# The entry of three FFNs: norm, sums of x, first weights and covered tiles put in one given order

## Chip, cores and metric

The kernel runs on one core of a Trainium2 chip. The metric is device time in microseconds of one execution of the whole program. TensorE (PE) multiplies matrices into PSUM banks, VectorE (DVE) and ScalarE (ACT) do elementwise work, GpSimd (POOL) and SyncE (SP) mostly issue transfers here.

## What is computed

A decoder trunk of two layers on 512 tokens of width 1024, all in float32:

```python
for l in range(DEPTH):                                   # DEPTH = 2
    x = x + 0.5 * swiglu(rms_norm(x, ffn1_norm[l]), ffn1_w_in[l], ffn1_w_out[l])
    h = rms_norm(x, mix_norm[l]) @ w_mix_in[l]           # three token mixers share this projection
    y = concat(short_conv(...), hgrn2(...), forgetting_attention(...))
    x = x + y @ w_mix_out[l]
    x = x + 0.5 * swiglu(rms_norm(x, ffn2_norm[l]), ffn2_w_in[l], ffn2_w_out[l])

def swiglu(h, w_in, w_out):                              # D_FF = 2816
    gate, up = jnp.split(h @ w_in, 2, axis=-1)
    return (jax.nn.silu(gate) * up) @ w_out
```

So there are four FFNs in the program: FFN1 and FFN2 of layer 0, FFN1 and FFN2 of layer 1. The two FFN2 stand directly behind a mixer; FFN1 of layer 1 stands behind FFN2 of layer 0. Only the first FFN has a different opening (it reads x from memory).

## The kernel before

**Numbers in two parts.** Every float32 operand of a matmul is kept as a high part (a copy rounded to float32r, made by ScalarE) and a low part (the rest, a subtraction on VectorE). A product is three matmuls: high x high, high x low, low x high (`mm3`, lines 327, 333, 334; its `hl` tiles hold weights, `x` or `xc` tiles the activations). Weights come in by transfers into `st` tiles (two buffers) or `w` tiles, and their two parts go into `hl` tiles (three buffers), by `granule` and `parted` (lines 315 and 316) or `prepare` (lines 696 and 698).

**Covered tiles and halved products.** The hidden width 2816 is 22 tiles of 128. At the start of an FFN the first tiles (6 in the first FFN, 4 in the other three) are computed plainly, in pairs: one covered pair is a `stream` over the 8 tiles of x's rows, in four granules of two row tiles each, 96 matmuls of 512 columns. They are called covered because beside them the norm and the operands of what follows are made. The rest is done by a scheme with seven products of half size in place of eight (named P1 to P7): `plan` writes the sequence of products and the steps between them, `halved` runs it, `product` is 24 matmuls of 256 columns. For it the activations are needed as quarters (4 tiles of x by 256 tokens), scaled by gain and the norm, and as sums of quarters; each of the seven has its own high and low part, `xc` (`halves_of_x`, lines 594, 600, 629 to 634). The sequence of an input product is P1, P2, P6, P5, P7, P3, P4; products use banks a, c, a, b, a, b, a, and ScalarE copies bank a (`g`) after P1 and P6 and bank b (`u`) after P5, before the bank is added to again.

**The norm.** The sum of squares (`sqa`) is brought across partitions by a matmul with `ones_mean` (line 427 in `norm`, called inside the first covered pair), then Ln, Exp, a square on ScalarE and three VectorE steps give `inv` (`end_norm`, `rsqrt`).

**What sets the order.** Tile dependencies give the waits. Beyond them a scheduler places instructions by priority, unless `follow` chains an instruction to the one before it on its engine ("a", "v", "p" and so on): chained instructions keep the order in which the code writes them. In `halved` all is chained. In the entry (`cover`, `halves_of_x`, `finish`) of before almost nothing is, and weight parts of covered tiles have high priority. `finish` turns a covered tile's two banks into its hidden values: two multiplies by `inv` (lines 554, 555), a silu, two multiplies into `hq` quarters (lines 573, 576).

**The split pass.** In every P1 of an input product the first matmul is done as two of 128 columns (`parted` in `mm3`), the rest as one of 256.

Of the kernel before, what the change touches and what calls it, by code (L numbers as in the profile page):

```python
# [8 lines left out]
F32 = mybir.dt.float32  # L9
F32R = mybir.dt.float32r  # L10
# [4 lines left out]
ALU = mybir.AluOpType  # L15
# [22 lines left out]

AHEAD_LOAD, AHEAD_SUM = 4, 4


# [17 lines left out]
def plan(covered):  # L59

    into = lambda c: [
# [15 lines left out]
    def between(a, b, *what):  # L82

        loose.append((max(a, 0), max(b, 0), what))
# [78 lines left out]
class Trunk:  # L163
# [32 lines left out]
    def build_consts(self, scratch):  # L196

        nc = self.nc
# [84 lines left out]
    def granule(self, parts, kk, ahead=True, skew=0):  # L283
# [14 lines left out]
        with self.tc.high_priority() if ahead else ExitStack():  # L298
            hi, lo = self.parted(st[:, : kk * c], 1 if ahead else kk, skew)
# [3 lines left out]
    def parted(self, src, pieces=1, skew=0):  # L303

        nc = self.nc
        n = src.shape[1]
        hl = self.wp.tile([P, 2 * 1024 + 64], F32R, tag="hl", name=self.n("hl"), bufs=3)  # L310
        hh, ll = (hl[:, a + skew : a + skew + n] for a in (0, 1024))
        w = n // pieces
        for c in range(0, n, w):
            hi, lo = hh[:, c : c + w], ll[:, c : c + w]
            a = nc.scalar.copy(hi, src[:, c : c + w])  # L315
            b = nc.vector.tensor_sub(lo, src[:, c : c + w], hi)  # L316
            if pieces > 1:
                self.follow("a", a)
                self.follow("v", b)
        return hh, ll  # L320

    def mm3(self, acc, ah, al, bh, bl, first, last, parted=False, keep=False):

        nc = self.nc
        n = bh.shape[-1]
        for c in (slice(0, n // 2), slice(n // 2, n)) if parted else (slice(0, n),):
            i = nc.tensor.matmul(  # L327
                acc[:, c], ah, bh[:, c], start=first and c.start == 0, stop=False,
                skip_group_check=True,
            )  # L330
            if keep:
                self.follow("p", i)
        nc.tensor.matmul(acc, ah, bl, start=False, stop=False, skip_group_check=True)  # L333
        i = nc.tensor.matmul(acc, al, bh, start=False, stop=last, skip_group_check=True)  # L334
        if keep:
            self.follow("p", i)
# [4 lines left out]

    def stream_steps(self, jobs, parts_of, act, nk, mid=None, pre=None):

        k = 0
        while k < nk:
# [5 lines left out]
            skew = SKEW_MOVING if jobs[0][2] is not None and jobs[0][0].shape[-1] < T else 0  # L359
            rows = self.granule(parts_of(k, kk), kk, pre is None, skew)  # L360
            end = k + kk == nk
# [30 lines left out]
    def norm_part(self, j, pool, xj=None, part=None):  # L392

        nc = self.nc
# [21 lines left out]

    def rsqrt(self, out, v, r, t):

        nc = self.nc
        self.act(t, r, AF.Square)  # L420
        nc.vector.scalar_tensor_tensor(out=t, in0=v, scalar=EPS, in1=t, op0=ALU.add, op1=ALU.mult)  # L421
        nc.vector.tensor_scalar(t, t, scalar1=-0.5, scalar2=1.5, op0=ALU.mult, op1=ALU.add)
        nc.vector.tensor_mul(out, r, t)

    def end_norm(self, bank, pool):
# [5 lines left out]
        self.act(r, bank, AF.Ln, bias=self.epsc)  # L431
        self.act(r, r, AF.Exp, scale=-0.5)
        self.inv = self.res.tile([P, T], F32, tag="inv", name=self.n("inv"))
        self.rsqrt(self.inv, bank, r, t)


    def ffn(self, w_in, w_out, next_gain, covered, begin=None, out=None):

        nc = self.nc
        tc = self.tc
        with tc.tile_pool(name=self.n("ffn"), bufs=1) as fp:
            self.tt, self.tb = "g2", 2
            if begin is not None:
                x, gain, logits = begin
            self.hq = {}
            halved = self.halved(fp, w_in, w_out, covered)
            finish = self.cover(fp, w_in, covered, begin, halved)
            for n, _ in enumerate(halved):  # L450

                if n in (1, 3):
                    finish(n // 2)

# [41 lines left out]
    def cover(self, fp, w_in, covered, begin, then):  # L496

        nc = self.nc
# [45 lines left out]

    def finish(self, fp, f, i, pg, pu, keep):

        nc = self.nc  # L550
# [3 lines left out]
        V(nc.vector.tensor_mul(gi, pg, self.inv))  # L554
        V(nc.vector.tensor_mul(ui, pu, self.inv))
        A(self.act(gi, gi, AF.Silu))
        a, k = divmod(f + i, 4)
        for b in range(2):
            V(self.hidden(self.quarter(fp, 0, a, b)[:, k, :], *(t[:, 256 * b : 256 * b + 256] for t in (gi, ui)), a != b))

    def quarter(self, fp, c, a, b):


        if (c, a, b) not in self.hq:
# [5 lines left out]
    def hidden(self, out, g, u, other):  # L570

        if other:
# [5 lines left out]
    def halves_of_x(self, fp):  # L578

        nc = self.nc
# [38 lines left out]
    def two(self, hi, lo, src, other):  # L624

        nc = self.nc
# [9 lines left out]
    def halved(self, fp, w_in, w_out, covered):  # L636

        nc = self.nc  # L650
# [5 lines left out]
        def src(u, q):  # L656

            kind, w = u
# [10 lines left out]
        def add(u, q, q2):  # L669

            G(nc.gpsimd.dma_start(raw[u, q], src(u, q2), accum_op=ALU.add))

        def total(u, name):

            q = lambda i: raw[u, i]
# [24 lines left out]
        def moving(c, p):  # L700

            hi, lo = (
# [42 lines left out]
        for q in (2, 0, 3, 1):  # L745
# [3 lines left out]
            S(nc.sync.dma_start(t, src(u, q)))  # L749
        add(u, 2, 3)  # L750
        yield
        total(u, "S2")
        for s in seq[: LEAD - 1]:
            prepare(*s)()
        run(-1)
# [10 lines left out]
        for n, (kind, w, p) in enumerate(seq):  # L766
# [68 lines left out]
    def lower_bounds(self, logits, scratch):  # L835

        nc = self.nc
# [53 lines left out]
    def mix(self, l, w, w_out, conv_w, out_gain, q_gain, k_gain, f_bias, next_gain):  # L891
# [3 lines left out]
        with tc.tile_pool(name=self.n("mix"), bufs=1) as mp:  # L895
# [23 lines left out]
            def features_steps(spans, banks, mid=None):  # L919

                bs = [self.bank(t) for t in banks]
# [13 lines left out]
            def tokens(a, banks=("mm", "mm")):  # L935

                bs = [self.bank(t) for t in banks]
# [78 lines left out]
            with tc.tile_pool(name=self.n("at"), bufs=1) as ap_:  # L1016
# [37 lines left out]
                def most():  # L1054

                    for dg in range(4):
# [52 lines left out]
    def hgrn(self, l, pr, hp, z, q, q2, v, sg, og):  # L1109

        nc = self.nc
# [175 lines left out]
    def fox_decay(self, mp, zf):  # L1293

        nc = self.nc
# [24 lines left out]
    def fox_qkv(self, mp, hf, tokens, half):  # L1320


        nc = self.nc
# [28 lines left out]
    def fox_prep(self, pool, h, qk, g):  # L1352

        nc = self.nc
# [106 lines left out]
    def turn_x(self):  # L1464

        nc = self.nc
# [15 lines left out]
    def open_x(self, x, gain, fp, k, loaded=False):  # L1482

        if not loaded:
# [16 lines left out]
    def load_x(self, x, j, fp):  # L1501

        nc = self.nc
# [10 lines left out]
def trunk_kernel(  # L1514
# [6 lines left out]
    for l in range(DEPTH):  # L1521
        k.ffn(
            ffn1_w_in[l], ffn1_w_out[l], mix_norm[l], 4 if l else 6,
            begin=(x, ffn1_norm[0], hgrn_lb_logits) if l == 0 else None,
# [38 lines left out]
```

## Time and profile before

| | us |
|---|---|
| median of 3 runs | 1865.98 |
| runs | 1869.36, 1865.98, 1865.92 |
| span of the profiled execution | 1868.0 |
| the run that can hold that span (the other two are shorter than it) | 1869.36 |
| TensorE busy | 1837.1 (98%) |
| VectorE busy | 1481.9 (79%) |
| ScalarE busy | 1009.8 (54%) |

A row of a profile's timeline gives the start, the length, the engine, the line of the kernel, the operation, what it writes and reads with their shapes, and in brackets how long the engine stood idle before it and what it then waited for. Matmuls overlap: the distance between two starts is the pace, not the length. A window row gives, for each stretch of time, busy time and count of instructions per engine, then the clock granted to TensorE (1.00 is full), the share of the transfer engines and GB/s.

### The profile page before, as it was taken

How to read it: one execution, taken by the hardware profiler on the slowest of the kernel's cores; microseconds unless marked ns; L12 is line 12 of the kernel's file. 1: busy time of each engine (PE TensorE's matmuls, PEld its weight loads, DVE VectorE, ACT ScalarE, POOL GpSimd, SP SyncE). 2: the span in 40 equal slices, each digit the busy share in tenths (PEclk: the TensorE clock that was granted, in tenths of full speed). 3: DMA queues.
4: the chain of work that ended last, by engine and by line, in shares of the span. 5: the costliest groups of instructions: out<-in, count | busy, mean ns of one | idle time of the engine just before them, and what ended most of it. 6: DMA issues, size and time to landing. Idle time of an engine off the chain costs nothing.

```text
span 1868.0 us, 33432 instructions
## 1 busy us (share of the span) xinstructions
PE 1837.1 (98%) x13559; PEld 1707.5 (91%) x13559; DVE 1481.9 (79%) x2101; ACT 1009.8 (54%) x1467; POOL 177.4 (9%) x182
## 2 busy tenths in 40 slices
PE   8999999999999999999999999999999999999999
PEld 6899999899878799999889999988998777999997
DVE  7889787677887978878697887867768878888883
ACT  4455554564676545555455555545547654555552
POOL 0011120100000011112001111201000000021210
PEclk9999999999999999999999999999999999999999
DMA  7658783332323757868265786823323237577662
GB/s 203 169 119 189 181 178 92 74 92 69 80 80 95 216 105 170 189 171 170 79 202 129 167 191 171 170 63 91 78 61 90 80 107 204 147 155 196 147 137 90
DMA packets 245418, 251.91 MB, mean 135 GB/s; under 512 B 19568, under 2 KB 230000, under 8 KB 245264
## 3 DMA queue, kind: packets, MB, share of 16 engines
q1 hardware_dynamic: 191664, 183.69, 33.1%
q0 software_dynamic: 53600, 66.09, 22.2%
q8 instruction: 106, 1.74, 0.4%
q14 instruction: 48, 0.39, 0.1%
HBM read 223.98 MB, written 2.10 MB: 121 GB/s over the span
## 4 chain that ended last, share of the span: by engine, by line
PE 85%; DVE 8%; ACT 3%; issue 2%; DMA 2%; SPq 0%; ACTq 0%; DVEq 0%
PE mm L327 12%; PE mm L334 12%; PE mm L333 12%; PE sc L327 6%; PE sc L334 6%; PE sc L333 6%; PE pt L327 6%; PE pt L333 6%; PE pt L334 6%; PE po L327 3%; PE po L333 3%; PE po L334 3%; DVE hl L316 1%; DMA st<-in_ffn_w_in_dram 1%; ACT hl L315 1%
## 5 line engine op out<-in xcount | busy, mean ns | idle before, releaser
L696 ACT CAST hl<-w 128x1024 fp32r<-128x1024 f32 x322 | 337.6, 1049 | 338.0 <-PE mm L334 80.7
L698 DVE TENSOR_TENSOR hl<-w,hl 128x1024 fp32r<-128x1024 f32 x322 | 392.9, 1222 | 104.9 <-ACT hl L696 104.9
L316 DVE TENSOR_TENSOR hl<-st,hl 128x512 fp32r<-128x512 f32 (+2 forms) x196 | 166.7, 852 | 117.6 <-ACT hl L315 116.4
L315 ACT CAST hl<-st 128x512 fp32r<-128x512 f32 (+2 forms) x196 | 146.6, 750 | 189.4 <-PE mm L334 67.8
L327 PE MATMUL mm<-xc,hl 128*128 128x256 f32 (+1 forms) x741 | 202.1, 276 | 1.1 <-ACT g L796 1.1
L333 PE MATMUL mm<-xc,hl 128*128 128x256 f32 x728 | 201.9, 277 | 0.0
L334 PE MATMUL mm<-xc,hl 128*128 128x256 f32 x728 | 201.2, 276 | 0.0
L334 PE MATMUL sc<-xc,hl 128*128 128x256 f32 x528 | 148.4, 281 | 8.7 <-DVE hl L698 8.7
L327 PE MATMUL sc<-xc,hl 128*128 128x256 f32 (+1 forms) x538 | 148.9, 280 | 0.6 <-ACT g L796 0.5
L333 PE MATMUL sc<-xc,hl 128*128 128x256 f32 x528 | 148.5, 281 | 0.0
L327 PEld LDWEIGHTS mm<-xc,hl 128*128 128x128 f32 x741 | 138.3, 188 | 1.6 <-ACT g L796 1.5
L334 PEld LDWEIGHTS mm<-xc,hl 128*128 128x128 f32 x728 | 136.9, 188 | 0.0
L333 PEld LDWEIGHTS mm<-xc,hl 128*128 128x128 f32 x728 | 136.7, 188 | 0.0
L327 PE MATMUL pt<-xc,hl 128*128 128x256 f32 (+1 forms) x488 | 133.1, 275 | 0.0
L333 PE MATMUL pt<-xc,hl 128*128 128x256 f32 x480 | 133.0, 277 | 0.0
L334 PE MATMUL pt<-xc,hl 128*128 128x256 f32 x480 | 132.6, 276 | 0.0
L327 PE MATMUL mm<-hl,x 128*128 128x256 f32 (+1 forms) x384 | 112.4, 293 | 1.0 <-DVE ft L421 0.4
L334 PEld LDWEIGHTS sc<-xc,hl 128*128 128x128 f32 x528 | 101.5, 192 | 9.1 <-DVE hl L698 9.1
L327 PE MATMUL mm<-x,hl 128*128 128x512 f32 x272 | 109.7, 403 | 0.0
L334 PE MATMUL mm<-hl,x 128*128 128x256 f32 (+1 forms) x384 | 107.5, 280 | 0.0
L333 PE MATMUL mm<-hl,x 128*128 128x256 f32 (+1 forms) x384 | 107.2, 279 | 0.0
L334 PE MATMUL mm<-x,hl 128*128 128x512 f32 x272 | 106.6, 392 | 0.0
(470 smaller groups left out, 5695.1 us busy)
## 6 DMA issues: line engine op xcount, KB each, us to landing
w<-in_ffn_w_in_dram SPq DMA_DIRECT2D x140, 512.0 KB, 5.2
w<-in_ffn_w_out_dram SPq DMA_DIRECT2D x64, 512.0 KB, 4.5
w<-in_ffn_w_out_dram POOLq DMA_DIRECT2D x56, 512.0 KB, 8.5
st<-in_w_mix_in_dram SPq DMA_DIRECT2D x88, 256.0 KB, 2.8
st<-in_ffn_w_in_dram SPq DMA_DIRECT2D x72, 256.0 KB, 3.2
w<-in_ffn_w_in_dram POOLq DMA_DIRECT2D x35, 512.0 KB, 8.1
w<-S POOLq DMA_DIRECT2D x35, 512.0 KB, 4.7
st<-in_ffn_w_out_dram SPq DMA_DIRECT2D x24, 512.0 KB, 3.6
```

The costliest lines, as they stand in the source:

```text
L315: a = nc.scalar.copy(hi, src[:, c : c + w])
L316: b = nc.vector.tensor_sub(lo, src[:, c : c + w], hi)
L327: i = nc.tensor.matmul(acc[:, c], ah, bh[:, c], start=first and c.start == 0, stop=False, skip_group_check=True,)
L333: nc.tensor.matmul(acc, ah, bl, start=False, stop=False, skip_group_check=True)
L334: i = nc.tensor.matmul(acc, al, bh, start=False, stop=last, skip_group_check=True)
L696: A(nc.scalar.copy(hi, src))
L698: return lambda: V(nc.vector.tensor_sub(lo, src, hi))
```

## The change

For the three FFNs other than the first, the entry is a new function, `enter`, in place of `cover` and `halves_of_x`. It does the same operations, and chains ScalarE's and VectorE's in the order written: the norm, then x's quarters and sums in the order P1, P2, P5, P6 with the weight parts of the second covered pair between them, then the first sum of weights and the first two products' weights. `stream_steps` gets a `given` argument: a granule for which it holds is chained, and the generator stops after making it, ahead of its matmuls. P7, P3, P4 and the covered tiles' hidden values are left for `entry`, a table by product number that `halved` calls behind its products (0, 1, 2, 3, 5, 6, 8, 9). The norm's matmul now stands after the third granule of the first covered pair, and the first four transfers of the halved products are issued ahead of the second pair's second granule. Apart from that, the first pass of P1 is split only at the first pair of each of the three chunks and at the first halved pair. `finish` is divided in `clear` and `values`.

```diff
+FIRST = 6
...
     def stream_steps(self, jobs, parts_of, act, nk, mid=None, pre=None, given=None):
...
+            keep = given is not None and given(k)
+            rows = self.granule(parts_of(k, kk), kk, pre is None, skew, keep)
+            if keep:
+                yield
...
+            if begin is None:
+                self.enter(fp, w_in, halved)
+                for _ in halved:
+                    pass
...
+    def enter(self, fp, w_in, then):
...
+        ba = self.next4()
+        first = stream(0, ba, lambda k: k == KD - 2)
+        for _ in range(4):
+            next(first)
+        nb = self.bank("pt" if self.ntog % 2 == 0 else "po")
+        bb = self.next4()
+        second = stream(2, bb, lambda k: True)
+        self.ngain = self.const.tile([P, KD], F32, tag="ngain", name=self.n("ngain"))
+        A(nc.scalar.activation(self.ngain, self.gain, AF.Copy, scale=-1.0))
+        next(second)
+        self.end_norm(nb, fp, True)
+        self.table(SILU)
+        next(first, None)
+        next(then)
...
+        quarter(0, 0)
+        high("P1")
+        quarter(1, 0)
+        lows["P1"]()
+        next(second)
+        next(second)
+        high("P2")
+        quarter(0, 1)
+        lows["P2"]()
+        quarter(1, 1)
+        add((0, 0), (0, 1))
+        high("P5")
+        next(second)
+        next(second)
+        clear(0, 0)
+        lows["P5"]()
+        add((0, 0), (1, 1))
+        high("P6")
+        next(second)
+        next(second)
+        next(second, None)
+        self.given["total"]()
+        lows["P6"]()
+        self.given["prepare"](0)
+        self.given["prepare"](1)
+        clear(0, 1)
+        add((0, 1), (1, 1))
+        next(then)
+        self.entry = {
+            0: lambda: (high("P7"), values(0, 0), lows["P7"]()),
+            1: lambda: (values(0, 1), high("P3")),
+            2: lambda: (lows["P3"](), add((0, 0), (1, 0))),
+            3: lambda: both("P4"),
+            5: lambda: clear(2, 0),
+            6: lambda: values(2, 0),
+            8: lambda: clear(2, 1),
+            9: lambda: values(2, 1),
+        }
...
-            product(u, p, acc, p in new, p in ("P2", "P3", "P4"), kind == "I" and p == "P1")
+            product(
+                u, p, acc, p in new, p in ("P2", "P3", "P4"),
+                kind == "I" and p == "P1" and w in (covered, *(f0 for f0, _ in CHUNKS)),
+            )
+            if n in self.entry:
+                self.entry.pop(n)()
```

In `enter`, `quarter` is four multiplies on VectorE, `high` a copy on ScalarE, `low` the rest on VectorE, `add` a sum of two quarters on VectorE, and `next(second)` alternately makes a granule's weight parts and issues its matmuls.

More of the change, by code (lines that the diff above doesn't have):

```diff
@@ L297, in granule, with parted @@
             at += w
[L298 to L299 removed]
+        with self.tc.high_priority() if ahead and not keep else ExitStack():
+            hi, lo = self.parted(st[:, : kk * c], 1 if ahead else kk, skew, keep)
         h3, l3 = (a.rearrange("p (k c) -> p k c", k=kk) for a in (hi, lo))
         return [(h3[:, i, :], l3[:, i, :]) for i in range(kk)]
[L303 removed]
+    def parted(self, src, pieces=1, skew=0, keep=False):
         nc = self.nc
@@ L415, in norm_part, with rsqrt, end_norm @@
             nc.vector.tensor_add(self.sqacc, self.sqacc, sq)
-    def rsqrt(self, out, v, r, t):
+    def rsqrt(self, out, v, r, t, keep=False):
         nc = self.nc
[L420 to L425, printed above, removed]
+        A, V = ((lambda i, e=e: self.follow(e, i)) if keep else (lambda i: i) for e in "av")
+        A(self.act(t, r, AF.Square))
+        V(nc.vector.scalar_tensor_tensor(out=t, in0=v, scalar=EPS, in1=t, op0=ALU.add, op1=ALU.mult))
+        V(nc.vector.tensor_scalar(t, t, scalar1=-0.5, scalar2=1.5, op0=ALU.mult, op1=ALU.add))
+        V(nc.vector.tensor_mul(out, r, t))
+    def end_norm(self, bank, pool, keep=False):
         nc = self.nc
@@ L430, in end_norm @@
         self.table(LNEXP)
-        self.act(r, bank, AF.Ln, bias=self.epsc)
-        self.act(r, r, AF.Exp, scale=-0.5)
+        A = (lambda i: self.follow("a", i)) if keep else (lambda i: i)
+        A(self.act(r, bank, AF.Ln, bias=self.epsc))
+        A(self.act(r, r, AF.Exp, scale=-0.5))
         self.inv = self.res.tile([P, T], F32, tag="inv", name=self.n("inv"))
-        self.rsqrt(self.inv, bank, r, t)
+        self.rsqrt(self.inv, bank, r, t, keep)
     def ffn(self, w_in, w_out, next_gain, covered, begin=None, out=None):
@@ L447, in ffn @@
             self.hq = {}
+            self.entry = {}
             halved = self.halved(fp, w_in, w_out, covered)
[L449 to L453, printed above, removed]
+            if begin is None:
+                self.enter(fp, w_in, halved)
+                for _ in halved:
+                    pass
+            else:
+                finish = self.cover(fp, w_in, covered, begin, halved)
+                for n, _ in enumerate(halved):
+                    if n in (1, 3):
+                        finish(n // 2)
             f0, nf = CHUNKS[-1]
@@ L556, in finish, with values @@
         A(self.act(gi, gi, AF.Silu))
+        return gi, ui
+    def values(self, fp, f, i, gi, ui, keep):
+        V = (lambda i: self.follow("v", i)) if keep else (lambda i: i)
         a, k = divmod(f + i, 4)
@@ L559, in finish, with stream, parts, quarter @@
             V(self.hidden(self.quarter(fp, 0, a, b)[:, k, :], *(t[:, 256 * b : 256 * b + 256] for t in (gi, ui)), a != b))
+    def enter(self, fp, w_in, then):
+        nc = self.nc
+        H = T // 2
+        A, V = (lambda i, e=e: self.follow(e, i) for e in "av")
+        def stream(f, banks, given):
+            def parts(k, kk):
+                r = slice(k * P, (k + kk) * P)
+                return [w_in[r, f * P : (f + 2) * P], w_in[r, FF + f * P : FF + (f + 2) * P]]
+            return self.stream_steps(
+                [(bk, slice(c, c + P), None) for bk, c in zip(banks, (0, 256, 128, 384))],
+                parts, self.xact, KD, given=given,
+            )
[13 more added lines that the diff above has]
+        next(then)
+        X, self.xc, lows = {}, {}, {}
+        def quarter(a, b):
+            X[a, b] = t = fp.tile([P, 4, H], F32, tag=f"r{2 + 2 * a + b}", name=self.n("xn"))
+            for k in range(4):
+                i = 4 * a + k
+                V(nc.vector.scalar_tensor_tensor(
+                    out=t[:, k, :], in0=self.xT[:, i, b * H : (b + 1) * H],
+                    scalar=(self.gain if a == b else self.ngain)[:, i : i + 1],
+                    in1=self.inv[:, b * H : (b + 1) * H], op0=ALU.mult, op1=ALU.mult,
+                ))
+        def high(name):
+            c = ORDER_IN.index(name)
+            src, other = X[SUM[name]], name in NEGATIVE
+            hi, lo = (
+                fp.tile([P, 4, H], F32R, tag=f"x{w}{c}", name=self.n("xc")) for w in "hl"
+            )
+            self.xc[name] = hi, lo
+            A(nc.scalar.activation(hi, src, AF.Copy, scale=-1.0) if other else nc.scalar.copy(hi, src))
+            def low():
+                V(nc.vector.scalar_tensor_tensor(
+                    out=lo, in0=src, scalar=-1.0, in1=hi, op0=ALU.mult, op1=ALU.subtract
+                ) if other else nc.vector.tensor_sub(lo, src, hi))
+            lows[name] = low
+        def add(x, y):
+            V(nc.vector.tensor_add(X[x], X[x], X[y]))
+        def both(name):
+            high(name)
+            lows[name]()
+        def row():
+            next(second)
+            next(second, None)
+        cleared = {}
+        def clear(f, i):
+            banks = bb if f else ba
+            cleared[f, i] = self.clear(fp, banks[2 * i], banks[2 * i + 1], True)
+        def values(f, i):
+            self.values(fp, f, i, *cleared.pop((f, i)), True)
+        quarter(0, 0)
[17 more added lines that the diff above has]
+        next(second)
+        next(second)
+        next(second, None)
+        self.given["total"]()
[15 more added lines that the diff above has]
+        }
@@ L750, in halved @@
         add(u, 2, 3)
+        self.given = {
+            "total": lambda: total(u, "S2"), "prepare": lambda i: prepare(*seq[i])(),
+        }
         yield
-        total(u, "S2")
-        for s in seq[: LEAD - 1]:
-            prepare(*s)()
+        if covered == FIRST:
+            total(u, "S2")
+            for s in seq[: LEAD - 1]:
+                prepare(*s)()
         run(-1)
```

12 lines of the change are left out of this document (7 added, 5 removed).

## Prediction

> **What bounds the kernel now.** I read the page first: shares, then the chain that ended last.
>
> ```profile
> span 1868.0 us, 33432 instructions
> ...
> PE 1837.1 (98%) x13559; PEld 1707.5 (91%) x13559; DVE 1481.9 (79%) x2101; ACT 1009.8 (54%) x1467; POOL 177.4 (9%) x182
> ...
> PE 85%; DVE 8%; ACT 3%; issue 2%; DMA 2%; SPq 0%; ACTq 0%; DVEq 0%
> ```
>
> TensorE is busy 98% of the span and holds 85% of the chain. So only two things move the time: fewer matmul slots, or less of what TensorE waits for. The second view is the list of TensorE's own waits.
>
> ```profile
> PE sc L334 <- DVE hl L698: 8.7, 2, 4.4
> ...
> PE po L327 <- DVE nt L421: 1.1, 1, 1.1
> PE mm L327 <- ACT g L796: 1.1, 2, 0.5
> ...
> PE sc L327 <- ACT g L796: 0.5, 1, 0.5
> ```
>
> The largest is two waits for VectorE's lower half of a weight tile (L698), 4.4 us each. The order of TensorE's instructions in time shows them, one at the first half-size product of each FFN that stands directly behind a mixer:
>
> ```profile
> 648.92 0.33 PE L327 MATMUL sc<-xc,hl 128*128 128x128 f32 x2
> 649.09 0.33 PE L333 MATMUL sc<-xc,hl 128*128 128x256 f32 x1
> 653.79 0.58 PE L334 MATMUL sc<-xc,hl 128*128 128x256 f32 x1 [4.37 <-DVE hl L698]
> ...
> 658.57 0.28 PE L327 MATMUL sc<-xc,hl 128*128 128x256 f32 x1
> ...
> 661.97 0.28 PE L327 MATMUL sc<-xc,hl 128*128 128x256 f32 x1
> ```
> ```profile
> 1569.52 0.33 PE L333 MATMUL sc<-xc,hl 128*128 128x256 f32 x1
> 1574.19 0.58 PE L334 MATMUL sc<-xc,hl 128*128 128x256 f32 x1 [4.35 <-DVE hl L698]
> ...
> 1580.10 0.28 PE L334 MATMUL sc<-xc,hl 128*128 128x256 f32 x1
> ```
>
> At full pace starts are 0.1133 us apart (30 from 658.57 to 661.97; the first two of a product, split or behind a split, 0.17). So 649.09 should have been followed at 649.26. 4.53 us are lost at 653.79 and 4.50 at 1574.19. Then the matmuls are slow: the 22 from 653.79 to 658.57 take 4.78 us where 22 x 0.1133 = 2.50 is normal (2.28 lost), the 27 from 1574.19 to 1580.10 take 5.91 for 3.06 (2.85 lost). The granted clock agrees: the stretches view gives it by window.
>
> ```profile
> 44.00:48.00 4.00, 2.88 (x13) 2.07 (x12) 2.45 (x5) 2.75 (x5) 0.00 (x0) 1.00 0.00 1
> ...
> 649.00:657.00 8.00, 3.63 (x19) 3.44 (x18) 7.00 (x9) 1.68 (x2) 1.55 (x2) 0.66 0.45 137
> 657.00:665.00 8.00, 8.00 (x66) 8.00 (x66) 4.51 (x5) 3.13 (x4) 0.65 (x1) 0.91 0.78 125
> 951.00:983.00 32.00, 32.00 (x145) 26.59 (x144) 30.83 (x43) 14.88 (x17) 0.83 (x2) 1.00 0.74 213
> 983.00:999.00 16.00, 15.47 (x136) 15.27 (x135) 12.35 (x17) 8.94 (x12) 1.38 (x2) 1.00 0.62 134
> ```
>
> It is 0.66 and 0.91 around the 4.4 us wait; around the 1.1 us wait for nt (in 44 to 48) it stays 1.00. A wait therefore costs extra clock somewhere between 1.1 and 4.4 us. The two entries behind mixers lose 4.53 + 2.28 + 4.50 + 2.85 = 14.16 us. The third FFN that the change touches is the second layer's first; its second covered pair and first products fill 951 to 983, and TensorE is busy all 32 us: no such wait. A little later in it (983 to 999, 15.47 of 16) stands one of the 0.5 us waits for ScalarE's g, and one (sc) in the second FFN. Counted from start to start a wait is 0.16 longer than the view's figure (4.53 beside 4.37), so these are 0.65 each, 1.3 together. Before: 15.5 us lost in three entries.
>
> **The change part by part.** *Fewer split passes.* In the built order 23 first passes of a product are one 256-wide matmul instead of two 128-wide ones; nothing else is added to or taken from any engine (the copies, sums and transfers have equal counts).
>
> ```profile
> 103.21 0.33 PE L327 MATMUL po<-xc,hl 128*128 128x128 f32 x2
> ...
> 103.66 0.28 PE L327 MATMUL po<-xc,hl 128*128 128x256 f32 x1
> ...
> 104.01 0.28 PE L327 MATMUL po<-xc,hl 128*128 128x256 f32 x1
> ```
>
> The triple with the pair takes 103.66 - 103.21 = 0.45, the next one without 0.35 (0.34 by its pitch). So 0.11 x 23 = 2.5 us, all on the path, since TensorE is the limit there. Bounds: 0 (were all 23 behind a wait) and 2.6.
>
> *The order at the entry.* VectorE and ScalarE now follow a list: sums in the order in which products want them, weights of the covered tiles between, P7, P3 and P4 pushed behind the first products. I work through the second FFN's entry with pitches from these rows.
>
> ```profile
> 627.16 0.39 PE L327 MATMUL mm<-x,hl 128*128 128x512 f32 x1
> ...
> 632.60 0.39 PE L327 MATMUL mm<-x,hl 128*128 128x512 f32 x1
> ```
> ```profile
> 621.71 0.69 ACT L270 ACTIVATE nr<-po,epsc 128x512 f32<-128x512 f32 x1 [2.13 <-issue]
> ...
> 623.23 0.63 ACT L270 ACTIVATE nr<-nr 128x512 f32<-128x512 f32 x1
> 623.89 0.63 ACT L270 ACTIVATE nt<-nr 128x512 f32<-128x512 f32 x1
> ...
> 627.36 1.06 ACT L315 CAST hl<-st 128x1024 fp32r<-128x1024 f32 x1 [1.53 <-PE pt L334]
> 628.31 1.06 ACT L629 ACTIVATE xc<-xn 128x1024 fp32r<-128x1024 f32 x1
> ```
> ```profile
> 626.54 1.67 DVE L594 SCALAR_TENSOR_TENSOR xn<-xT,gain,inv 128x256 f32<-128x256 f32 x4
> 628.13 0.87 DVE L594 SCALAR_TENSOR_TENSOR xn<-xT,ngain,inv 128x256 f32<-128x256 f32 x2
> ...
> 635.16 1.22 DVE L316 TENSOR_TENSOR hl<-st,hl 128x1024 fp32r<-128x1024 f32 x1
> 636.30 1.22 DVE L600 TENSOR_TENSOR xn<-xn,xn 128x1024 f32<-128x1024 f32 x1
> ...
> 643.11 0.68 DVE L554 TENSOR_TENSOR gi<-sc,inv 128x512 f32<-128x512 f32 x1
> 643.71 1.21 DVE L630 SCALAR_TENSOR_TENSOR xc<-xn,xc 128x1024 fp32r<-128x1024 f32 x1
> ```
>
> Pitches: four 256-wide multiplies of x 1.59 (628.13 - 626.54), a 1024-wide operation on VectorE 1.14, a 512-wide 0.60, a 1024-wide copy on ScalarE 0.95 and 1.05 until it is done, 24 matmuls of a granule 5.44 (632.60 - 627.16).
>
> Step 1. Ln, Exp and the square no longer have a weight copy between them. Exp stood 623.23 - 621.71 = 1.52 behind Ln; without the copy it is 0.69 + 0.03 (the 0.03 from 623.23 + 0.63 to 623.89). The first multiply starts 0.80 earlier, at 625.74.
>
> Step 2. VectorE's list is then 16 multiplies, four 1024-wide steps (lower P1, one weights, lower P2, one sum): 6.36 + 4.56, sum done at 636.74. ScalarE's queue holds the copy of P5, waiting for that sum, and **behind it** the copy of the weights for rows 4 and 5 of the second covered pair: P5 from 636.78, weights from 637.73 to 638.78. TensorE is there at 627.16 + 2 x 5.44 = 638.04. New wait: 0.8.
>
> Step 3. VectorE goes on with lower weights, two 512-wide, lower P5, a sum: from 638.82 to 643.52. P6's copy, then the last weights: done at 645.56. TensorE is there at 638.84 + 5.44 = 644.28. New wait: 1.35.
>
> Step 4. The first product starts at 645.62 + 5.44 = 651.06, where it was 648.92. Its lower half, the wait of before, is VectorE's fourth 1024-wide step after 645.6: done near 650.2, 0.9 us of cover. That stall goes.
>
> Step 5. What is late next: VectorE has 1024-wide work for every product plus the sums that were pushed back. Continuing the list, the fourth product ends at 662.05; the fifth needs ScalarE's copy of the first bank (g), queued behind a weight copy that waits for VectorE's sum of weights (658.9): done 662.33, wait 0.35. The sixth needs the copy u, queued behind P4, whose sum ends at 663.62: done 666.15, TensorE there at 665.11, wait 1.1. Then 0.4 at the next pair.
>
> So each entry loses 0.8 + 1.35 + 0.35 + 1.1 + 0.4 = 4.0 us, none of it as long as the waits of before. All three entries get the list, the third too, which lost only 0.65: 3 x 4.0 = 12.0 against 15.5. Gain 3.5.
>
> *Transfers.* On SP's queue the four 512 KB weight loads of the first product now stand ahead of two covered granules; before they followed them.
>
> ```profile
> L749 SPq DMA_DIRECT2D w<-in_ffn_w_in_dram x4: 368/500/507, 620.6 to 622.1; - x4
> ...
> L671 POOL DMA_DIRECT2D w<-in_ffn_w_in_dram x2: 1339/1488/1637, 625.6 to 656.0; - x2
> ```
> ```profile
> 626.00:627.00 1.00, 1.00 (x6) 0.81 (x5) 0.96 (x3) 0.00 (x0) 0.98 (x1) 1.00 1.10 347
> 630.00:631.00 1.00, 1.00 (x6) 0.82 (x5) 1.00 (x4) 0.03 (x1) 0.00 (x0) 1.00 1.23 198
> ```
>
> Before, they were issued at 620.6 behind the last sum of squares. VectorE's new list ends that sum earlier; I take 618.4. Four issues of 0.5, two of 0.4, and 2.6 MB at 347 GB/s (7.6 us) bring the granule in near 627.1; ScalarE wants it at 628.3. Covered by 1.2 us, so I take nothing; without that cover it costs one for one. The row at 630 moves 198 GB/s only, after POOL's accumulating transfer (issued at 625.6) has joined, and at that rate the granule would be 4 us late.
>
> *Other moves.* ngain, a copy of eight columns that ScalarE did early, goes into the list ahead of the norm, where ScalarE is idle: nothing.
>
> **The sum.** -2.5 - 15.5 + 12.0 = -6.0. The profiled execution spans 1868.0; of the runs shown only 1869.36 is above that, so I take 1.4 around it and get 1863.4 for an execution like it. The median, 1865.98, stands 3.4 lower; nothing ties that to the entries, so I take the same 6.0 off: **1860.0 us**. Were it one or both clock losses missing in those runs (2.28 to 2.85 each), the gain would be 2.6 to 3.5.
>
> Errors: five waits an entry, each good to about 0.25, give 3 x 1.2 = 3.7 either way if all err together; the split passes 0 to 2.6.
>
> **The rivals.** *1. The clock drops at the new waits.* The 1.35 follows the 0.8 by one granule; between 1.1 and 4.4 the trace tells nothing. Slow matmuls would cost 2.28 to 2.85 an entry, of which the 0.35 and 1.1 of step 5 are taken back (TensorE arrives later): about 1.1 net, 3 x 1.1 = 3.3, time 1863.3. Against: 44 to 48 holds 1.00. [...]
>
> *2. Slower: the granule behind the four loads lands late.* At 198 GB/s it lands at 632.5, 4 us after ScalarE's turn; the copy holds VectorE's list one for one, the wait at 638 grows from 0.8 to 5, long enough for the clock. An entry then loses 4.0 + 4.2 + 1.1 = 9.3; three 28, time 1866.0 - 2.5 - 15.5 + 28 = 1876. It decides from an entry loss of (15.5 + 2.5) / 3 = 6.0, about 2 us beyond the cover. For it: the row at 630. Against: the accumulating transfer needs two of those loads first.
>
> *3. The list moves the stall, not shortens it.* Every step for TensorE stays as late as VectorE's total says: the sums are as many as before, and if VectorE's work ahead of the fifth product sets the pace, only the split passes are left: 1863.5.
>
> **How the numbers follow.** Forecast 0.68, rival 1 0.14, rival 2 0.10, rival 3 0.08. The measurement tells apart about 0.2%, 3.7 us. The forecast's own range, 1856 to 1864, lies under 1862.3 in about five of six: 0.57, with some of rivals 1 and 3, 0.60 faster. Same takes the rest of them, 0.30; slower, rival 2, 0.10. The range 1855.5 to 1866.0 takes in the errors, the two rivals at 1863 and the case of clock losses missing from the median, and leaves out rival 2 and the tails.
>
> **What would show it.** Right: no wait of TensorE for the lower half of L698's successor above 1 us; in each of three entries a wait near 0.65 and one near 1.2 us on the second covered pair, for ScalarE's weight copy (the view subtracts some 0.16 from start to start); granted clock 1.00 around them; first product about 2 us later behind the norm; 24 128-wide matmuls instead of 70. Wrong: a clock below 1.00 in the windows of the entries (rival 1), ScalarE waiting for st there (rival 2), waits over 6 us in an entry.

## The result

The changed kernel takes 1863.49 us (median of 19 runs, 1861.58 to 1865.24) where the kernel before takes 1867.36 (19 runs, 1865.60 to 1869.36). The ratio is 0.9979, 95% interval 0.9972 to 0.9986: 3.9 us less, between 2.6 and 5.2. A later set (experiment 5) gave 0.9965 (0.9953 to 0.9978), so 6.5 us less, between 4.1 and 8.8. The forecast was 6.0 less, 1860.0, in a range from 1855.5 to 1866.0.

The page of the changed kernel (span, busy time and number of instructions, then the chain that ended last):

```profile
span 1861.1 us, 33375 instructions
PE 1832.9 (98%) x13536; PEld 1700.2 (91%) x13536; DVE 1480.2 (80%) x2101; ACT 1006.0 (54%) x1467; POOL 177.3 (10%) x182
PE 87%; DVE 7%; ACT 3%; issue 2%; DMA 1%; SPq 0%; ACTq 0%; DVEq 0%
```

TensorE has 23 instructions fewer (13536 for 13559; 24 matmuls of 128 columns in x's products where there were 70), VectorE and ScalarE as many as before. TensorE's waits, from its list (engine, line, what for; total, times, longest):

```profile
PE mm L308 <- ACT hl L297: 3.8, 4, 1.1
PE sc L308 <- ACT hl L297: 2.1, 3, 1.1
PE pt L308 <- ACT u L877: 1.7, 2, 0.8
...
PE mm L308 <- ACT u L877: 0.8, 1, 0.8
...
PE pt L308 <- ACT g L874: 0.4, 2, 0.2
...
PE po L308 <- ACT g L874: 0.2, 1, 0.2
```

The two waits of 4.4 us for VectorE's lower half of a weight tile are gone. In their place stand short ones for ScalarE: for its weight copy (L297) two in each of three entries (the seventh in the list, 0.3 us, is in the first FFN), and for its copies u and g behind the first products. TensorE's instructions in time show them; the first five rows are the second FFN, the next two the second layer's first, the last two its second:

```profile
636.74 0.39 PE L315 MATMUL po<-x,hl 128*128 128x512 f32 x1
637.92 0.50 PE L308 MATMUL mm<-x,hl 128*128 128x512 f32 x1 [0.79 <-ACT hl L297]
644.80 0.50 PE L308 MATMUL mm<-x,hl 128*128 128x512 f32 x1 [1.14 <-ACT hl L297]
650.37 0.34 PE L308 MATMUL sc<-xc,hl 128*128 128x128 f32 x2
665.36 0.39 PE L308 MATMUL pt<-xc,hl 128*128 128x256 f32 x1 [0.83 <-ACT u L877]
968.41 0.50 PE L308 MATMUL sc<-x,hl 128*128 128x512 f32 x1 [0.69 <-ACT hl L297]
975.28 0.50 PE L308 MATMUL sc<-x,hl 128*128 128x512 f32 x1 [1.10 <-ACT hl L297]
1556.36 0.50 PE L308 MATMUL mm<-x,hl 128*128 128x512 f32 x1 [0.80 <-ACT hl L297]
1563.23 0.50 PE L308 MATMUL mm<-x,hl 128*128 128x512 f32 x1 [1.10 <-ACT hl L297]
```

The stretches view of the same place, where the clock stood at 0.66 and 0.91 before, and of the second layer's first FFN:

```profile
649.00:657.00 8.00, 8.00 (x66) 7.75 (x65) 8.00 (x11) 5.01 (x6) 2.20 (x2) 1.00 0.74 198
657.00:665.00 8.00, 7.53 (x65) 7.17 (x63) 8.00 (x9) 5.30 (x7) 0.00 (x0) 1.00 0.44 72
951.00:983.00 32.00, 30.22 (x140) 24.50 (x139) 25.30 (x36) 14.04 (x16) 1.68 (x2) 1.00 0.65 186
```

The clock is 1.00 throughout. In the second layer's first FFN TensorE is busy 30.22 of 32 us where it had no gap before: that entry pays for the list, the two behind mixers gain by it.

### The profile page after: what moved, and what is told of

It reads as the page before. It is cut to its first block, busy times and chain, and to the rows that moved or that the text cites. A ratio compares the mean times of both kernels' runs of the same rounds, so it can differ in the third digit from the quotient of the medians.

```text
span 1861.1 us, 33375 instructions
## 1 busy us (share of the span) xinstructions
PE 1832.9 (98%) x13536; PEld 1700.2 (91%) x13536; DVE 1480.2 (80%) x2101; ACT 1006.0 (54%) x1467; POOL 177.3 (10%) x182
## 4 chain that ended last, share of the span: by engine, by line
PE 87%; DVE 7%; ACT 3%; issue 2%; DMA 1%; SPq 0%; ACTq 0%; DVEq 0%
PE mm L308 13%; PE mm L315 12%; PE mm L314 12%; PE sc L308 6%; PE sc L314 6%; PE sc L315 6%; PE pt L308 6%; PE pt L314 6%; PE pt L315 6%; PE po L308 3%; PE po L314 3%; PE po L315 3%; DVE hl L298 1%; DVE xn L576 1%; ACT hl L297 1%
## 5 line engine op out<-in xcount | busy, mean ns | idle before, releaser
L297 ACT CAST hl<-st 128x512 fp32r<-128x512 f32 (+2 forms) x196 | 146.5, 750 | 183.3 <-PE mm L315 67.6
L315 PE MATMUL sc<-xc,hl 128*128 128x256 f32 x528 | 146.2, 277 | 0.0
L314 PE MATMUL sc<-xc,hl 128*128 128x256 f32 x528 | 146.1, 277 | 0.0
L308 PE MATMUL mm<-x,hl 128*128 128x512 f32 x272 | 110.2, 405 | 3.8 <-ACT hl L297 3.8
L314 PE MATMUL mm<-x,hl 128*128 128x512 f32 x272 | 106.1, 390 | 0.0
L315 PE MATMUL mm<-x,hl 128*128 128x512 f32 x272 | 105.3, 392 | 0.0
```

The lines of the kernel that those rows point to most:

```text
L308: i = nc.tensor.matmul(acc[:, c], ah, bh[:, c], start=first and c.start == 0, stop=False, skip_group_check=True,)
```

## The experiments

**1. Was the profiled execution of before an unusual one?** The pair of profiles differs by 6.9 us (1868.0 to 1861.1), the medians by 3.9. The nearest suspect was the clock: two half-clock stretches that the median execution might not have.

> The kernel before, unchanged, for a second profiled execution. In the first, span and launch came to 1869.9 us (1868.0 and the 1.9 by which the runs stand above their spans), 2.5 above the median of 1867.36, and it held two stretches at half clock (6.83 us each, 2.3 to 2.9 us lost each) behind the two waits of 4.4 us. Theory A: the usual execution lacks one or both of these stretches, so the change can gain only 3.1 to 3.7 us against it, as measured (3.9). Then this profile has a span near 1865.5 and one half-clock stretch or none at the two FFNs behind mixers, with both waits of 4.4 us still there. Rival B: the clock losses are in every execution, and the shortfall lies elsewhere. Then both stretches are there again, whatever the span. Time against before: 1.000.

Measured: 1868.23 beside 1868.63 in the same set, ratio 1.0001 (0.9992 to 1.0010); span 1867.2. The stretches view, cut at the changes of the clock:

```profile
649.96:653.37 3.41, 0.00 (x0) 0.00 (x0) 3.41 (x6) 1.04 (x1) 0.00 (x0) 1.00 0.85 287
653.37:656.79 3.42, 3.00 (x14) 3.00 (x15) 2.63 (x3) 0.00 (x0) 1.34 (x2) 0.50 0.01 4
656.79:660.20 3.41, 3.41 (x32) 3.41 (x32) 1.08 (x1) 1.55 (x2) 0.86 (x1) 1.00 0.92 163
```

At this entry half clock lasts 3.42 us instead of 6.83 and costs 0.8 us less; at the other it is 6.83 again. And the granted clock over the span is known for each execution: it lies between 0.996 and 0.998 in all 64 executions of before that ran with the experiments (the 11 of this one among them). In 52 of the 64 it is 0.997 or less, which is more than 9 us at half clock. In the first profile 1.2 us of that is a last drop behind the final matmul (from 1866.78 to the end of the span), and the longest single stretch in a kept profile is 6.83 us. So the usual execution has more than one stretch, as the three kept profiles with the old entries have one at each entry behind a mixer (before, this one, and experiment 2's). Theory A falls as an account of the median; what varies is the length of the loss. In the 12 executions at 0.998 the mean alone does not tell two short stretches from one long one. Of the 19 executions of the changed kernel 16 show 1.000 and three 0.999, which is 1.9 to 5.6 us at half clock; no trace of these three is kept, so where it lies is not known. What else varies between executions of the same code is told under experiment 5.

**2 and 3. The two parts alone.** The split passes alone, in the kernel before:

```diff
-            product(u, p, acc, p in new, p in ("P2", "P3", "P4"), kind == "I" and p == "P1")
+            product(u, p, acc, p in new, p in ("P2", "P3", "P4"),
+                    kind == "I" and p == "P1" and w in (covered, *(f0 for f0, _ in CHUNKS)))
```

> The kernel before with the first pass of P1 split once a chunk alone; the entries are left as they were. By the sum 23 x 0.11 = 2.5 us less, ratio 0.9987 (theory A and B). Rival C: the split passes are worth nothing outside the profile, and the measured 3.9 us come from the entries alone: ratio 1.000. Its profile is a third sample of the entries of before: A expects the half-clock stretch missing in some of them, B two stretches.

Measured: ratio 0.9988 (0.9979 to 0.9997), 2.2 us less, with the waits of before:

```profile
PE sc L334 <- DVE hl L698: 8.7, 2, 4.4
```

Its profile has both half-clock stretches too (3.41 and 6.83 us), and yet it spans 1861.1 us, exactly as the changed kernel's does. The span of one execution does not tell what an entry is worth.

And the entries alone, in the changed kernel:

```diff
-                kind == "I" and p == "P1" and w in (covered, *(f0 for f0, _ in CHUNKS)),
+                kind == "I" and p == "P1",
```

> The changed kernel with the first pass of every P1 split as before: the entries alone. The profiles give 12.8 us lost in the three entries after (4.3 each) and 15.5 to 16 before: 3.5 us less, ratio 0.9981, if the profiled execution of before is typical (B). A: 3.9 - 2.5 = 1.4 us less, ratio 0.9993, as the usual execution of before loses one clock stretch less. Rival C: 3.9 us less, 0.9979.

Measured: ratio 0.9987 (0.9979 to 0.9996), 2.4 us less, between 0.7 and 3.9. The 2.5 of the split passes lies in its interval and nothing does not (C falls by experiment 2). For the entries 3.5 lies inside the interval, and so do the 1.4 of A and the 3.9 of C, so this time does not tell them apart; A fell by the clock. The table under experiment 4 has a sharper measure.

**4. The third entry left as it was.** The sum said that the list costs in the entry that does not stand behind a mixer.

```diff
+            self.listed = begin is None and listed
...
-            if begin is None:
+            if self.listed:
                 self.enter(fp, w_in, halved)
...
-        if covered == FIRST:
+        if not self.listed:
             total(u, "S2")
...
         k.ffn(
             ffn1_w_in[l], ffn1_w_out[l], mix_norm[l], 4 if l else FIRST,
+            listed=False,
```

> The changed kernel, but the FFN that does not stand behind a mixer (first of the second layer) keeps the old entry. That entry lost 0.65 us before and 4.3 after in the profiles, so it should be 3.5 us faster than the changed kernel: 7.4 us under before, ratio 0.9960. If the new list cost nothing there outside the profile, 3.9 us under before, 0.9979.

Measured: ratio 0.9955 (0.9942 to 0.9967), 8.4 us less than before. That is 4.5 more than the changed kernel's 3.9 of the first set and 1.9 more than its 6.5 of the later one, with 3.5 expected; between sets the medians do not settle it. The profiles do. The table has the time from the seventh matmul of an entry's first covered pair to the start of its fifteenth halved product, read off TensorE's starts: the same matmuls in every row, but for one split pass an entry (0.11 us).

| us, in the profile of | second FFN | second layer's first | second layer's second |
|---|---|---|---|
| before | 89.21 | 82.22 | 89.33 |
| before again (experiment 1) | 88.43 | 82.23 | 89.33 |
| entries alone (experiment 3) | 85.96 | 85.54 | 85.95 |
| changed kernel | 85.65 | 85.85 | 85.65 |
| this run | 85.67 | 82.09 | 85.67 |
| weights first (experiment 6) | 82.52 | 82.52 | 82.52 |

The entries behind mixers win 2.8 to 3.7 us each; the one that had no long stall loses 3.6, and the old entry gives them back. With the split passes alike (experiment 3 against the two profiles of before) the three entries together win 3.3 us, or 2.5 against the profile in which one half-clock stretch of before was short.

**5. The changed kernel again.**

> The changed kernel unchanged, beside the other runs of this call, for a second interval and profile. Theory A2: the 6.0 us of the sum (3.5 for the entries, 2.5 for the split passes) are right, and 3.9 +- 1.3 was low by the scatter of single executions (some 2 us either way): ratio 0.9968 to 0.9976. Rival: one of the two terms is smaller outside the profiled executions: 0.9979 again.

Measured: 0.9965 (0.9953 to 0.9978). The 6.0 of the sum lies in this interval; in that of the first set, which ends at 5.2, it does not. Profiled executions of the same code show what moves by itself. One thing is TensorE's pace at full clock (granted 1.00 in the windows 1208 to 1238 of the first two profiles here and 1209 to 1239 of the third). Here are pairs of rows from before (nine matmuls apart), from the first profile of the changed kernel (nine) and from the second (six), all of the same stretch of FFN1 of the second layer:

```profile
1212.77 0.28 PE L334 MATMUL mm<-xc,hl 128*128 128x256 f32 x1
...
1213.83 0.28 PE L334 MATMUL mm<-xc,hl 128*128 128x256 f32 x1
```
```profile
1212.84 0.28 PE L308 MATMUL mm<-xc,hl 128*128 128x256 f32 x1
...
1213.86 0.28 PE L308 MATMUL mm<-xc,hl 128*128 128x256 f32 x1
```
```profile
1208.72 0.28 PE L314 MATMUL sc<-m,hl 128*128 128x256 f32 x1
...
1209.43 0.28 PE L314 MATMUL sc<-m,hl 128*128 128x256 f32 x1
```

The pace is 0.118, 0.113 and 0.118 us. The slow pace lasts some 23 us here and costs 1.0 us, without a wait, in one profile of the changed kernel and not in the other. Matmul by matmul the second profile falls 2.7 us behind the first: 0.75 at the program's opening, 1.85 in three such stretches, and 0.1 in all the rest, the waits of the entries among it. The length of half clock (0.8 us) is another thing that moves. A third may be a transfer in the second mixer, some 1.2 us on the path in the three profiles with the old split passes and in none of the eight with the new ones (the row "PE pt L1155 <- ACT t L270: 0.5, 1, 0.5" of before is part of it); whether that is chance or an effect of the split passes was not tried. These are of the size of the scatter of single runs (1865.6 to 1869.4 before). Entries (3.3) and split passes (2.5) make 5.8 of the 6.9 between the first pair of profiles; the transfer is about as long as the rest.

**6 and 7. Two neighbours exchanged.** The new waits of 0.8 and 1.35 us were put down to ScalarE's queue: a weight copy behind a copy that waits for a sum. Rows of VectorE and of ScalarE in the changed kernel, second FFN:

```profile
634.63 1.21 DVE L599 TENSOR_TENSOR xn<-xn,xn 128x1024 f32<-128x1024 f32 x1
637.90 1.22 DVE L298 TENSOR_TENSOR hl<-st,hl 128x1024 fp32r<-128x1024 f32 x1 [2.06 <-ACT hl L297]
...
641.50 1.23 DVE L599 TENSOR_TENSOR xn<-xn,xn 128x1024 f32<-128x1024 f32 x1
644.78 1.23 DVE L298 TENSOR_TENSOR hl<-st,hl 128x1024 fp32r<-128x1024 f32 x1 [2.06 <-ACT hl L297]
```
```profile
628.49 1.05 ACT L589 CAST xc<-xn 128x1024 fp32r<-128x1024 f32 x1
635.88 1.05 ACT L589 CAST xc<-xn 128x1024 fp32r<-128x1024 f32 x1 [6.33 <-DVE xn L599]
636.83 1.04 ACT L297 CAST hl<-st 128x1024 fp32r<-128x1024 f32 x1
```

ScalarE stands idle 6.33 us with the weight copy queued behind P5's copy; then VectorE stands idle 2.06 us for the weight copy, and so again at P6. That is 4.1 us of VectorE an entry.

```diff
-        high("P5")
         next(second)
         next(second)
+        high("P5")
...
-        high("P6")
         next(second)
         next(second)
+        high("P6")
```

> The changed kernel with two neighbours exchanged in ScalarE's list, twice: the copy of the covered pair's weights ahead of P5's copy, and ahead of P6's. Theory T1: the waits of 0.8 and 1.35 come from that order alone. VectorE stood idle 2.06 us twice an entry, because ScalarE began the weight copy only after the copy that waits for VectorE's sum; these 4.1 us come back, so the waits of 0.35 and 1.1 behind go as well, and of 4.3 us an entry about 0.5 is left: 3 x 3.8 = 11 us under the changed kernel (1852.5, ratio to before 0.992). Rival T2 (the list only moves the stall): the sums as a whole are late, and the waits turn up at the first products again: within 1 us of the changed kernel. Rival T3: the weights are not there yet (buffer or transfer), so that the copy ahead holds back P5 and P6: slower than the changed kernel.

Measured: 1852.17 us, ratio to before 0.9908 (0.9895 to 0.9922), and 10.6 under the changed kernel's 1862.75 in the same set, with 11 expected. The same two engines now:

```profile
634.76 1.22 DVE L599 TENSOR_TENSOR xn<-xn,xn 128x1024 f32<-128x1024 f32 x1
635.89 1.22 DVE L298 TENSOR_TENSOR hl<-st,hl 128x1024 fp32r<-128x1024 f32 x1
...
639.48 1.23 DVE L599 TENSOR_TENSOR xn<-xn,xn 128x1024 f32<-128x1024 f32 x1
640.62 1.22 DVE L298 TENSOR_TENSOR hl<-st,hl 128x1024 fp32r<-128x1024 f32 x1
```
```profile
631.19 1.05 ACT L297 CAST hl<-st 128x1024 fp32r<-128x1024 f32 x1 [1.51 <-DMA st<-in_ffn_w_in_dram]
636.01 1.05 ACT L589 CAST xc<-xn 128x1024 fp32r<-128x1024 f32 x1 [3.77 <-DVE xn L599]
...
638.35 1.04 ACT L297 CAST hl<-st 128x1024 fp32r<-128x1024 f32 x1
```

VectorE has no gap left between sum and lower weights. ScalarE does meet a transfer that is not there yet (1.51 us, T3's mechanism), but 4.8 us before P5's sum is done, so it costs nothing. T2 falls: the sums were not late by VectorE's total, but by the two gaps.

The exchange at P5 alone:

> The exchange at P5 alone. T1: the first VectorE gap of 2.06 us goes; the wait of 0.8 goes with it, and that of 1.35 too, since all behind comes 2 us earlier. The second gap stays, so the waits of 1.1 and 0.4 stay: 1.6 of 4.3 us an entry, 8 us under the changed kernel (1855.5, ratio to before 0.9935). T2: no change.

Measured: 1855.35, ratio 0.9924 (0.9912 to 0.9937), 7.4 under the changed kernel, with 8 expected. Of TensorE's waits in the entries those for ScalarE's u are left, as forecast:

```profile
PE pt L308 <- ACT u L877: 1.6, 2, 0.9
...
PE mm L308 <- ACT u L877: 0.8, 1, 0.8
```

**8 and 9. From which wait on does the clock drop?** The wait for the last granule of the second covered pair was made longer by extra copies on ScalarE, in the kernel of experiment 7. The diff shows the added lines; its comment, which is not in the code, gives how many of the four tiles each extra copy takes, entry by entry.

```diff
         high("P6")
+        for n in self.extra.pop(0):     # (4, 4), (4, 4, 2), (4, 4, 4); in 9: (4, 2) three times
+            A(nc.scalar.copy(self.xc["P6"][0][:, :n, :], X[SUM["P6"]][:, :n, :]))
         next(second)
```

> The exchange at P5 alone, and ahead of the weight copy behind P6's ScalarE makes P6's copy again: twice in the first of the three entries, two and a half times in the second, three times in the third (nothing of the result changes). So TensorE gets one single wait at the last granule, of about 2.4, 3.0 and 3.5 us in the three entries. What is asked is from which wait on the granted clock drops, which the profiles of before and after leave open between 1.3 and 4.4 us. If the length alone decides with a bound of about one 3.4 us stretch (the half-clock times of before are 3.41 or 6.83 us long): 1.00 in the first two entries, a half-clock stretch in the third at most. If any wait clearly above 1.4 us is enough: a stretch in all three, 1.5 to 2.3 us more each. Without any: 2.4 + 3.0 + 3.5 + 3 x 0.4 = 10 us lost, 3 us under the changed kernel (1860.5); with three stretches 1865 to 1867.

Measured: 1866.05, ratio 0.9980 (0.9970 to 0.9989), granted clock from 0.996 to 0.999 in the ten runs. The time is inside the 1865 to 1867 expected for three half-clock stretches, but the profile has two, and in its first entry a wait of 1.1 us for VectorE that was not expected. The first two entries (waits of 2.7 and 3.1 us counted from start to start) each have a half-clock stretch, and the third, with the longest wait (3.6), has none. Length alone does not decide. The half-clock stretches begin whole multiples of 3.413 us after the clock's first record: 186 and 283 of them in this profile, 187 and 457 in that of before. The 3.413 is read off the stretches' starts on the span: (1573.24 - 651.64) / (457 - 187) in before, (978.70 - 647.61) / (283 - 186) here. Cut on that grid, the first and the third entry:

```profile
644.19:647.61 3.42, 1.28 (x6) 1.07 (x7) 1.30 (x2) 3.39 (x5) 0.00 (x0) 1.00 0.85 278
647.61:651.02 3.41, 3.41 (x10) 2.65 (x9) 3.41 (x4) 0.56 (x1) 0.00 (x0) 0.50 0.49 168
...
1562.38:1565.79 3.41, 1.86 (x9) 1.20 (x7) 0.00 (x0) 3.31 (x4) 0.00 (x0) 1.00 0.84 264
1565.79:1569.20 3.41, 1.64 (x7) 1.37 (x8) 1.66 (x2) 3.41 (x4) 0.00 (x0) 1.00 0.47 162
```

In the first, an interval in which TensorE was busy 1.28 of 3.41 us is followed by one at half clock; the third entry's wait lies across a grid line, with 1.86 and 1.64 busy, and the clock stays.

> As in the kernel of long waits, but P6's copy is made again one and a half times in each of the three entries, so that TensorE has one wait of about 2.0 to 2.2 us in each. The profiles so far show half-clock stretches that begin on a grid of 3.413 us counted from the first record; of nine waits from 2.7 to 4.6 us the one that did not drop the clock (3.6 us) lay astride a grid line, with 1.5 us on one side and 1.8 on the other, and each of the others had 2.1 us or more within one interval. Theory G: the clock drops when TensorE stands idle for more than some 1.8 to 2.1 us within one such interval. Then a wait of 2.1 us drops it only where it lies nearly whole in one interval: in the profile each entry can be told from its place, and the executions differ among themselves, from none to three stretches (granted clock 1.000 to 0.997). Rival L: the length alone decides, with a bound between 1.4 and 2.7 us: all three entries alike, in every execution. Time: 2.1 x 3 and the waits behind (0.1 + 1.1 + 0.4 each) give 11 us lost, 2 us under the changed kernel without a stretch, about equal to it with one.

Measured: 1864.25, ratio 0.9975 (0.9965 to 0.9985). Granted clock in nine runs: 1.000 twice, 0.999 three times, 0.998 four times. The first two entries of the profile, on the grid:

```profile
642.38:645.79 3.41, 1.60 (x8) 1.02 (x7) 0.17 (x1) 3.35 (x5) 0.00 (x0) 1.00 0.93 307
645.79:649.20 3.41, 3.41 (x9) 2.64 (x10) 3.41 (x4) 1.69 (x2) 0.00 (x0) 0.50 0.68 211
973.47:976.88 3.41, 1.70 (x8) 1.32 (x8) 1.60 (x2) 3.38 (x5) 0.00 (x0) 1.00 0.81 256
976.88:980.30 3.42, 3.42 (x17) 2.84 (x16) 3.42 (x4) 0.27 (x1) 0.00 (x0) 1.00 0.53 164
```

In the third entry the clock dropped too: 0.50 from 1563.98, behind the interval from 1560.56 with TensorE busy 1.60. By the view the three waits are 1.81, 1.71 and 1.82 us, and the one of 1.71 has no drop. Each lies whole within one interval, so this profile alone would also fit rival L, with a bound between 1.71 and 1.81. Rival L falls by the third entry of experiment 8: its 3.3 us by the view (3.6 from start to start) were far above any such bound and had no drop. The intervals with 1.60 of 3.41 us busy were followed by half clock, those with 1.64 (experiment 8) and 1.70 were not.

## Why the prediction was right, and where it was off

*The split passes*: 2.5 forecast, 2.2 measured (0.6 to 3.9). *The stalls of before*: gone, as step 4 said, and the clock losses with them. *What comes in their place*: the five waits of an entry were forecast at 0.8, 1.35, 0.35, 1.1 and 0.4. Counted from start to start, with the slower first matmul behind each, the second FFN shows 1.06, 1.41, 0.24, 1.11 and 0.48, together 4.3 for the forecast 4.0. The first sits at 637.92: 637.92 - 636.74 is 1.18 where 0.23 is normal. The first product starts at 650.37 (forecast 651.06); the entry as a whole stands 0.9 us earlier than before (its seventh matmul at 604.78 for 605.67), and from there the covered part takes 45.59 us where the forecast has 651.06 - 605.67 = 45.39. *The third entry*: it loses 3.6 us more than before, where the sum has 4.0 - 0.65 = 3.35, and experiment 4 gives them back. *The entries together*: 3.5 forecast; 3.3 and 2.5 by the table, 2.4 (0.7 to 3.9) by the medians of experiment 3.

*Rival 1* (clock) falls: 1.00 in all three entries, in both profiles of the changed kernel. The two waits start 6.9 us apart, so no interval of the grid holds both, and in the interval with the longer one TensorE was busy 2.42, 2.69 and 2.31 of 3.41 us in the three entries (from 643.81, 971.49 and 1562.00). The most that was followed by half clock in experiments 8 and 9 is 1.60. *Rival 2* (late granule) falls: ScalarE copies that granule at 627.55 right behind its copy of P1, without a wait for st. *Rival 3* (stall only moved) falls by the table, and with experiment 6. The time alone would not have told: 1863.49 lies beside the 1863.3 of rival 1 and the 1863.5 of rival 3, nearer than to 1860.0, and neither of them happened. That it lies in the range owes something to the range's width.

The step that was off is the last, from the sum to the median. The three runs shown then, with 1865.98 in the middle, were a low sample of a kernel whose median over 19 is 1867.36. So 6.0 less would have been 1861.4, not 1860.0; the other 2.1 of the miss are in the gain, 3.9 (2.6 to 5.2) in one set and 6.5 (4.1 to 8.8) in the other. The table and the split passes speak for 5.0 to 5.8; nearer than that it stays open. (The launch was set at 1.4 us where the changed kernel's profiled run has 1863.05 - 1861.1 = 1.95; the 1860.0 does not hang on it.) The case kept for a low median (a clock loss missing from the median runs, gain 2.6 to 3.5) came near the first number for a wrong reason, as experiment 1 showed.

The sum was also read too narrowly: its own step 2 names the weight copy queued **behind** P5's copy, and prices it at 0.8 us. The order cost 10.6 / 3 = 3.5 us an entry, because it delays VectorE and with it everything up to the sixth product.

## What to carry to other kernels

Where an engine's order is given, put the instruction whose input comes first ahead of the one that waits for another engine: two exchanges of neighbours were worth 10.6 us, more than the new entry itself. Use a new order only where the old one stalls; here one of three places lost half of what the other two had won (3.6 of some 7). And a pair of profiles with a scatter of 2 us each is no measure of a change of 4: take the terms from the profile and the total from many runs.

## What the hardware showed that was not expected

On the grid of experiment 8 (3.413 us, counted from the clock's first record) these intervals at full clock were followed by half clock: those with TensorE busy 0.02 and 1.20 us in before, 0.00 in experiment 1, 0.88 and 1.28 in experiment 8, and 1.60 twice in experiment 9. Intervals with 1.64 and 1.86 (experiment 8), 1.70 (experiment 9) and 2.31, 2.42 and 2.69 (the entries of the changed kernel) were not. These are single intervals of five profiles; what holds between 1.60 and 1.64, or in another kernel, was not shown. Once at half clock, 1.26 and 2.46 us busy (before, from 651.64 and 1573.24) were followed by another such interval, 3.00 (experiment 1) by full clock. So a wait of 2.7 us (first entry of experiment 8) cost about another 1.6, where one of 3.6 across a grid line cost nothing more. The 1.6 is an estimate: starts at half clock were 0.425 us apart in that profile (978.98 to 979.83, two matmuls), at full clock 0.227, so 3.41 us at half clock hold 8.0 matmuls that take 1.8 at full. And executions of one kernel differ: granted clock 1.000 to 0.998 in the nine of experiment 9. Before, on the same grid:

```profile
648.22:651.64 3.42, 1.20 (x7) 0.86 (x5) 3.42 (x5) 1.30 (x2) 0.00 (x0) 1.00 0.52 141
651.64:655.05 3.41, 1.26 (x6) 1.26 (x7) 3.41 (x6) 1.04 (x1) 0.00 (x0) 0.50 0.47 166
655.05:658.46 3.41, 3.41 (x18) 3.41 (x18) 0.95 (x1) 0.00 (x0) 2.20 (x2) 0.50 0.52 96
...
1569.82:1573.24 3.42, 0.02 (x1) 0.00 (x0) 3.42 (x6) 1.11 (x2) 0.00 (x0) 1.00 0.93 285
```

A wait of 4.4 us, wherever it lies on such a grid, leaves at least one interval idle for 2.2 us, more than the 1.81 that half clock followed in experiment 9; and each of the 64 executions of before has such a loss (granted clock 0.998 at most).
